# A second set of weight buffers for six panels of a gated linear unit

## The chip, the cores and the metric

The kernel runs on one core of one Trainium2 chip. The metric is device time in microseconds for one execution of the whole program, as the median of several runs. Engines that matter here are TensorE (PE in the profile, with PEld for its weight loads), VectorE (DVE), ScalarE (ACT), GpSimd (POOL) and the engine that issues transfers (SP).

## The reference

Two layers of a decoder trunk, sequence length 256, width 2048, all in float32. The first layer mixes tokens with an S5 state-space model, the second with a causal convolution module; both are followed by a SwiGLU feed-forward block. The change lies in the first layer, in the gated linear unit behind the S5 model:

```python
y = jax.nn.gelu(y + d_skip.astype(f32) * u.astype(f32)).astype(u.dtype)
vg = y @ w_glu                       # (256, 2048) @ (2048, 4096)
return vg[..., :d] * jax.nn.sigmoid(vg[..., d:])
```

Around each sub-layer stands `x <- LayerNorm(alpha * x + (1 + gate(c)) * sublayer(x * (1 + scale(c)) + shift(c)))`. The six vectors shift, scale and gate of a layer are the product of an activated vector `c` with a matrix of 2048 x 12288, so these conditioning weights have to be read from HBM as well, beside the weights of the layers.

## The kernel before

Every large product is made of panels, and a panel of units. A unit is a piece of 512 of the 2048 inner rows by 512 output columns of a weight matrix (1 MB). For the gated linear unit a panel is 256 columns of the value half and the matching 256 of the gate half; there are eight panels of four units.

The path of a unit (class `Unit`): `load_unit` takes a tile named `raw` and SP issues two transfers of 512 KB into it (L585). ACT casts it to the high half `whi` (L843), and DVE subtracts that from `raw` to make the low half `wlo` (L844). PE multiplies: 16 matmuls with `whi` (activations high and low), 8 with `wlo` (L902). `whi` and `wlo` have two buffers each. A panel's last unit is taken in two halves, one for each output bank. At the end of a panel ACT and DVE form the gate (`sg`), PE transposes it (`turned`, L919), and DVE adds it into the residual `X` (L1074).

Beside this runs `AdaQueue`: at a rate of about one step per unit it loads a conditioning row block of 1 MB into a tile named `rawa` (L686, issued by SP), and DVE adds it, scaled, into `adaacc` (L699 and L701). When a vector is complete, PE sums it over partitions (`adar`, L709) and turns it (`adat`, L717).

`raw` and `rawa` tiles come from one pool, `rawp`, of four buffers of 1 MB:

```python
rawp = ctx.enter_context(tc.tile_pool(name="raw", bufs=4))
...
raws = [rawp]
...
    r = raws[0].tile([P, 4, 512], F32, tag="raw", name="raw")
...
    raws.append(raws.pop(0))
```

`raws` is a list of pools; each weight load takes a tile from the first and moves that to the end of the list. `rawa` tiles always come from `rawp`. SP's queue is worked off in order; a transfer whose buffer is not free yet holds up what stands behind it. A planner puts the instructions of each engine in an order: it goes by program order, and takes by its own estimate of time the first that is ready. Only the PE order of panel 0 is written out by hand.

Before panel 0 ends, the S5 model's tiles in the fast memory are given up (`s5.work_ctx.close()` and `s5.mats_ctx.close()` in `s5_end`). The room is next used by the pool `f0`, opened ahead of panel 7, whose one large tile first holds the split input of the feed-forward block (`entry_raw`, class `Entry`, L974 to L981) and later the block's inner activations. `reuse_waits="tile"` says that a tile of a pool laid over older tiles waits for those tiles it lies on.

The loop over the eight panels is at L1551 and the lines behind it.

Of the kernel before, what the change touches and what calls it, by code (L numbers as in the profile page):

```python
# [504 lines left out]
def kernel(  # L505
# [11 lines left out]
    rawp = ctx.enter_context(tc.tile_pool(name="raw", bufs=4))  # L517
# [4 lines left out]
    def aux(name):  # L522
        return auxp.tile([P, 512], F32, tag="aux", name=name)
# [51 lines left out]
    raws = [rawp]  # L575
# [495 lines left out]
    def residual(y, gt, ch, stats=None):  # L1071

        for k in range(2):
            done = nc.vector.scalar_tensor_tensor(  # L1074
                out=X[:, ch + k], in0=y[:, k], scalar=gt[:, ch + k:ch + k + 1], in1=X[:, ch + k], op0=MUL, op1=ADD)
            if stats and stats.behind:
                with queue_behind([done]):
                    stats.behind.pop(0)()
        if stats is None:
            return  # L1080
        i, z = ch // 2, X[:, ch:ch + 2]
        if i == 0:
            later.put(1, lambda: stats.begin(z))
            later.put(1, lambda: stats.add(0, z))
            for p in range(1, 8):
                later.put(1 if p == 1 else 2 + p % 2, lambda p=p: stats.move(X[:, 2 * p:2 * p + 2]))
        elif i == 1 and later.todo:
            later.put(1, lambda: stats.add(1, z))
        else:
            stats.add(i, z)  # L1090

    def gated(wsrc, off, width, sp, then, entry=None, wide=True, **kw):

        segs = [(off, 256), (width + off, 256)]
        if entry:
            def from_entry(vs):
                for i in range(2):
                    entry_gated(vs[i], vs[2 + i], sp)
                then(vs[0][2])

            entry.panel(wsrc, segs, [(256, 256), (width + 256, 256)], kw["wp"], from_entry)
            ada.credit = -3.0
            return
        acc = gemm(wsrc, 0, NCH, segs, xh, banks=((0, 2), (1, 3)), wide=wide, **kw)
        t = sp.tile([P, 2, SEQ], F32, tag="sg", name="sg", bufs=2)
        for i, ab in enumerate(acc):
            nc.scalar.activation(out=t[:, i], in_=ab[:, 1], func=AF.Sigmoid)
            nc.vector.tensor_tensor(out=t[:, i], in0=ab[:, 0], in1=t[:, i], op=MUL)
        if wide:
            turning.put(2, lambda: turned([t[:, 0], t[:, 1]], 0, then))  # L1110
        else:
            then(t)
# [9 lines left out]
    def gu_cols(f):  # L1122
        return [(f * P, 256), (DFF + f * P, 256)]
# [399 lines left out]
    def entry_raw(fp):  # L1523
        t = fp.tile([P, 24, 2, SEQ], F32R, tag="f2", name="raw").rearrange("p a h b -> p (a h b)")
        return t[:, 0:2 * NCH * EW]
# [5 lines left out]
    with mctx:  # L1531
# [4 lines left out]
        def enter(name, stats, i, k, raw, pairs):  # L1536

            layer, j = (i, 3) if k == 0 else (i + 1, 0)
            ada.finish(layer, j)
            ada.finish(layer, j + 1)  # L1540
            g, b = ln_gb(i, k)
            hg, hb = fold(name, g, b, mod[layer][:, j + 1], mod[layer][:, j])
            e = Entry(sp, stats, raw, hg, hb, scaled(name + "xg", g, ALPHA), scaled(name + "xb", b, ALPHA))
            for p in range(pairs):
                later.put(1 + p // 2, lambda p=p: e.split(p))
            return e

        f0ctx = ExitStack()
        bank = auxp.tile([P, 512], F32, tag="ada", name="acc", bufs=1)
        first = {"acc": [b.rearrange("p (a b) -> p a b", b=SEQ) for b in (aux("acc"), bank)], "before": {1: last_scan, 2: lambda: held_back.append(s5.end), 3: s5_end}}  # L1550
        for i in range(8):  # L1551
            if i == 7:
                fp = f0ctx.enter_context(tc.tile_pool(name="f0", bufs=1, reuse_waits="tile"))
                raw = entry_raw(fp)
                entry = enter("f0", stats, 0, 0, raw, 7)
            with ExitStack() as order:
                if i == 0:
                    order.enter_context(tc.manual_schedule(engines={mybir.EngineType.PE}))
                gated(s5_w_glu[0], 256 * i, D, sp, lambda t, i=i: residual(t, mod[0][:, 2], 2 * i, stats), wp=wp, wide=i < 7,
                      ahead=(ffn_w_gu[0], gu_cols(0)) if i == 7 else None, **(first if i == 0 else {}))  # L1560
            if i == 1:
                held_back.clear()
            ada.rate = 1.05
            ada.hold = i == 6
            if i == 0:
                later.put(10, load_vectors)
# [237 lines left out]
```

## Time and profile before

| | us |
|---|---|
| median of 3 runs | 2275.47 |
| lowest and highest run | 2272.48, 2278.56 |
| profiled execution, its own time | 2271.02 |
| its span | 2269.2 |
| panels 1 to 6 in it, first matmul of panel 1 to first of panel 7 | 230.3 to 376.4 |
| PE busy in the span | 2212.5 |
| DVE busy | 1669.2 |
| ACT busy | 1018.8 |
| mean rate of the transfers over the span | 255 GB/s |

A row of a timeline gives the start, the time, the engine, the line of the kernel, the operation, what it writes and reads, the shapes and how many instructions were merged; a bracket at the end is idle time of that engine just before, and what ended it. SPq is SP's queue, and a row there is the issue of a transfer, not the transfer. A row of waits gives the total, the number of times and the longest. In the table of stretches each engine has its busy time with the number of instructions.

### The profile page before, as it was taken

The page shows a single profiled execution, that of the slowest core. Times are in us where ns is not written, and L with a number is a line of the kernel's source. Part 1 is how long each engine was busy: PE and PEld are TensorE (multiplying, and loading weights), DVE is VectorE, ACT ScalarE, POOL GpSimd, SP SyncE. Part 2 cuts the span into 40 slices and gives each one's busy share as a digit, 9 for nine tenths or more (in the row PEclk, how much of TensorE's full clock was granted, in tenths as well). Part 3 has the DMA queues.
Part 4 walks back from the last instruction along what each step waited for, and adds up shares of the span by engine and source line. Part 5 has one row for each costly group of instructions (what it writes and reads, how often), then busy time and mean ns, then how long its engine had stood idle before and what let it go on. Part 6 is the DMA issues. An engine that isn't in the chain of part 4 may idle for free.

```text
span 2269.2 us, 33415 instructions
## 1 busy us (share of the span) xinstructions
PE 2212.5 (97%) x13611; PEld 1798.0 (79%) x13611; DVE 1669.2 (74%) x1812; ACT 1018.8 (45%) x1238; POOL 157.4 (7%) x265
## 2 busy tenths in 40 slices
PE   7999999999999999999999998999999999999998
PEld 4556778988788888787897776898888888888888
DVE  8897898878777777777988788878755444555474
ACT  4775334644333333333455434556443333434343
POOL 5761000000000000000010110000000000000000
PEclk8999999999999999999999999999999999999999
DMA  9998899589998899998856775757865555555542
GB/s 332 343 324 276 300 355 310 178 314 324 316 330 322 319 329 326 317 324 318 311 161 198 227 211 198 252 196 235 284 223 186 185 190 191 188 191 186 189 165 92
DMA packets 380607, 579.48 MB, mean 255 GB/s; under 512 B 13875, under 2 KB 277939, under 8 KB 365987
## 3 DMA queue, kind: packets, MB, share of 16 engines
q1 hardware_dynamic: 379862, 576.82, 74.9%
q8 instruction: 107, 1.75, 0.3%
q0 software_dynamic: 352, 0.45, 0.1%
q14 instruction: 46, 0.38, 0.1%
q10 hardware_dynamic: 240, 0.08, 0.0%
HBM read 573.72 MB, written 3.57 MB: 254 GB/s over the span
## 4 chain that ended last, share of the span: by engine, by line
PE 75%; DVE 11%; DMA 7%; ACT 4%; issue 2%; SPq 0%; POOL 0%; POOLq 0%; DVEq 0%; ACTq 0%
PE acc L902 61%; PE acc L907 6%; DMA raw<-in_ffn_w_gu_dram 4%; DVE wlo L844 3%; ACT whi L843 2%; PE acc L1019 2%; PE turned L919 2%; DMA raw<-in_s_w_glu_dram 1%; DVE adaacc L701 1%; PE conv L1695 1%; DMA raw<-in_ada_w_dram 1%; PE ada L629 1%; PE y L499 1%; DVE pin L476 1%; PE adar L709 0%
## 5 line engine op out<-in xcount | busy, mean ns | idle before, releaser
L844 DVE TENSOR_TENSOR wlo<-raw,whi 128x2048 fp32r<-128x2048 f32 x344 | 788.9, 2294 | 467.4 <-ACT whi L843 462.8
L843 ACT CAST whi<-raw 128x2048 fp32r<-128x2048 f32 x344 | 655.5, 1906 | 814.6 <-PE acc L902 414.6
L902 PE MATMUL acc<-whi,h 128*128 128x512 f32 x3648 | 890.4, 393 | 7.9 <-ACT whi L843 7.6
L902 PEld LDWEIGHTS acc<-whi,h 128*128 128x128 f32 x3648 | 678.6, 188 | 160.7 <-ACT whi L843 12.8
L902 PE MATMUL acc<-wlo,h 128*128 128x512 f32 x1824 | 461.7, 390 | 0.8 <-DVE wlo L844 0.5
L902 PEld LDWEIGHTS acc<-wlo,h 128*128 128x128 f32 x1824 | 341.6, 188 | 73.9 <-DVE wlo L844 3.3
L902 PE MATMUL acc<-whi,f 128*128 128x512 f32 x1248 | 300.9, 391 | 0.0
L701 DVE SCALAR_TENSOR_TENSOR adaacc<-rawa,c_act,adaacc 128x2048 f32<-128x2048 f32 (+1 forms) x135 | 284.6, 2108 | 0.4
L902 PEld LDWEIGHTS acc<-whi,f 128*128 128x128 f32 x1248 | 232.8, 188 | 49.5 <-ACT whi L843 1.7
L902 PE MATMUL acc<-wlo,f 128*128 128x512 f32 x624 | 156.5, 389 | 0.0
L902 PEld LDWEIGHTS acc<-wlo,f 128*128 128x128 f32 x624 | 117.1, 188 | 24.4
L1625 POOL TENSOR_TENSOR lw<-fold,wtap 128x1024 f32<-128x1024 f32 x12 | 26.6, 2220 | 1056.6 <-PE acc L907 867.7
L629 PE MATMUL ada<-raw,c_rep 128*32 128x512 f32 (+1 forms) x576 | 68.9, 574 | 7.0 <-DMA raw<-in_ada_w_dram 4.9
L1256 ACT ACTIVATE fsg<-acc 128x256 f32<-128x256 f32 x84 | 31.6, 379 | 96.1 <-PE acc L902 96.1
L907 PE MATMUL acc<-h,whi 128*128 128x256 f32 x512 | 66.8, 285 | 3.4 <-ACT h L923 2.5
L907 PEld LDWEIGHTS acc<-h,whi 128*128 128x128 f32 x512 | 63.2, 191 | 8.0 <-ACT h L923 4.5
L1198 POOL CAST lnmh<-lno 128x2 fp32r<-128x2 f32 x1 | 0.2, 181 | 883.6 <-DVE lno L68 883.6
L1257 DVE TENSOR_TENSOR fsg<-acc,fsg 128x256 f32<-128x256 f32 x84 | 35.0, 419 | 15.5 <-ACT fsg L1256 15.5
L1695 PE MATMUL conv<-vs,lw 128*32 128x256 f32 x720 | 42.2, 381 | 0.1
L907 PE MATMUL acc<-f,whi 128*128 128x256 f32 x320 | 40.8, 284 | 0.0
L907 PEld LDWEIGHTS acc<-f,whi 128*128 128x128 f32 x320 | 39.4, 192 | 0.2
L476 DVE TENSOR_TENSOR_SCAN pin<-rho,pin 128x1024 f32<-128x1024 f32 x16 | 36.7, 2295 | 0.6
(352 smaller groups left out, 1831.0 us busy)
## 6 DMA issues: line engine op xcount, KB each, us to landing
raw<-in_ffn_w_gu_dram SPq DMA_DIRECT2D x352, 512.0 KB, 4.7
rawa<-in_ada_w_dram SPq DMA_DIRECT2D x128, 1024.0 KB, 5.5
raw<-in_ffn_w_down_dram SPq DMA_DIRECT2D x88, 1024.0 KB, 5.1
raw<-in_ada_w_dram SPq DMA_DIRECT2D x64, 1024.0 KB, 8.0
raw<-in_s_w_glu_dram SPq DMA_DIRECT2D x64, 512.0 KB, 5.8
raw<-in_cv_w_pw_dram SPq DMA_DIRECT2D x64, 512.0 KB, 5.6
raw<-in_cv_w_pw_dram SPq DMA_DIRECT2D x16, 1024.0 KB, 5.7
vs<-scr SPq DMA_DIRECT2D x40, 142.0 KB, 5.5
```

The costliest lines, as they stand in the source:

```text
L476: done = v.tensor_tensor_scan(out=z, data0=rh.rearrange("p q r c -> p (q r c)"), data1=z, initial=0.0, op0=MUL, op1=ADD)
L629: nc.tensor.matmul(acc[32 * (k % 4):32 * (k % 4) + 32, :], c_rep[:, kk, :], r[:, k, :], start=kk < 4, stop=kk >= NCH - 4)
L701: nc.vector.scalar_tensor_tensor(out=acc, in0=r[:, i], scalar=c_act[:, kk:kk + 1], in1=acc, op0=MUL, op1=ADD)
L843: m1 = nc.scalar.copy(out=self.hi[:, :kn], in_=r[:, :kn])
L844: m2 = nc.vector.tensor_tensor(out=self.lo[:, :kn], in0=r[:, :kn], in1=self.hi[:, :kn].bitcast(F32), op=SUB)
L902: nc.tensor.matmul(acc[bank].rearrange("p a b -> p (a b)"), x[:, bank * HALF:(bank + 1) * HALF], wt[:, k], start=first, stop=end)
L907: nc.tensor.matmul(acc[bank][:, i], wt[:, k, m * P:(m + 1) * P], x, start=first and i == 0, stop=end and i == 1)
L919: nc.tensor.transpose(b[:, o:o + HALF], u[t][:, c0 + k * P:c0 + (k + 1) * P], ident)
L1019: nc.tensor.matmul(acc[m][:, 0:EW], wt[:, k, m * P:(m + 1) * P], xx[:, 4 * u + k], start=u == 0 and n == 0, stop=u == 3 and n == len(order ...
L1256: nc.scalar.activation(out=t[:, i], in_=gv[:, 0], func=AF.Sigmoid)
L1257: nc.vector.tensor_tensor(out=t[:, i], in0=gv[:, 0], in1=t[:, i], op=MUL)
L1695: nc.tensor.matmul(acc[32 * q:32 * q + 32, :], lw[:, q, g, :], vs[:, q, 4 * g:4 * g + SEQ], start=g == 0, stop=g == n - 1)
```

## The change

Ahead of panel 1 a pool of four buffers, `raw6`, is opened in the room that the S5 model has left, and the list of pools becomes six entries long: the old pool twice, the new one four times. Ahead of panel 7 the list is set back to the old pool, the new one is closed, and `f0` is opened as before. Nothing else differs.

```diff
         first = {"acc": [b.rearrange("p (a b) -> p a b", b=SEQ) for b in (aux("acc"), bank)], "before": {1: last_scan, 2: lambda: held_back.append(s5.end), 3: s5_end}}
+        wide_raws = ExitStack()
         for i in range(8):
+            if i == 1:
+                raws[:] = [rawp] * 2 + [wide_raws.enter_context(tc.tile_pool(name="raw6", bufs=4, reuse_waits="tile"))] * 4
             if i == 7:
+                raws[:] = [rawp]
+                wide_raws.close()
                 fp = f0ctx.enter_context(tc.tile_pool(name="f0", bufs=1, reuse_waits="tile"))
                 raw = entry_raw(fp)
                 entry = enter("f0", stats, 0, 0, raw, 7)
```

## The prediction

> **What bounds the kernel now.** The page came first, for the whole run. Its span and its counts:
>
> ```profile
> span 2269.2 us, 33415 instructions
> PE 2212.5 (97%) x13611; PEld 1798.0 (79%) x13611; DVE 1669.2 (74%) x1812; ACT 1018.8 (45%) x1238; POOL 157.4 (7%) x265
> ```
>
> PE is busy in 2212.5 of 2269.2 us, so all that any prefetch can win in the whole run is 57 us, and most of that lies outside the stage that the change touches. The next view is busy time by stretch, cut at the first matmul of panel 1 (230.3), of panel 2 (253.4) and so on to panel 7 (376.4), with one stretch behind it; columns are the stretch, its length, the busy time of PE, PEld, DVE, ACT and POOL (with instruction counts), the granted clock, the share of DMA time and GB/s.
>
> ```profile
> 230.30:253.40 23.10, 23.10 (x105) 19.15 (x104) 23.03 (x25) 9.12 (x9) 0.00 (x0) 1.00 0.94 324
> 253.40:280.40 27.00, 24.82 (x105) 18.34 (x103) 19.92 (x17) 9.29 (x8) 0.00 (x0) 1.00 0.98 342
> 280.40:305.70 25.30, 24.87 (x117) 19.26 (x116) 23.51 (x26) 9.06 (x8) 2.56 (x5) 1.00 0.92 321
> 305.70:328.70 23.00, 22.88 (x100) 18.25 (x100) 20.68 (x15) 8.80 (x8) 0.00 (x0) 1.00 1.00 339
> 328.70:352.30 23.60, 22.94 (x101) 18.27 (x101) 20.80 (x15) 8.83 (x8) 0.00 (x0) 1.00 1.02 363
> 352.30:376.40 24.10, 23.96 (x112) 18.72 (x112) 20.69 (x14) 10.53 (x9) 0.00 (x0) 1.00 1.01 350
> 376.40:400.00 23.60, 23.60 (x200) 23.60 (x198) 19.00 (x32) 14.72 (x25) 0.00 (x0) 1.00 0.75 240
> ```
>
> Panels 1 to 6 take 146.1 us, and PE idles there 0 + 2.18 + 0.43 + 0.12 + 0.66 + 0.14 = 3.53 us. Three things are nearly full at once: PE, DVE in panels 1 and 3, and the DMA engines from panel 4. The list of waits over 230.3 to 376.4 (total us, times, longest) says where a late weight goes:
>
> ```profile
> ACT whi L843 <- DMA raw<-in_s_w_glu_dram: 46.7, 17, 4.4
> ...
> PEld acc L902 <- ACT whi L843: 5.5, 7, 2.6
> ```
>
> ACT's cast to `whi` waits 46.7 us for weights, in 17 of the units, but ACT has that much slack: PE's weight loads, which run ahead of its matmuls, wait for it 5.5 us, and PE itself only in the two places shown below.
>
> **The wait that costs.** The timelines of PE, ACT, SP's queue and DVE around the longest one (start, length, instruction; in brackets the idle time before it):
>
> ```profile
> 253.44 3.79 PE L902 MATMUL acc<-whi,h 128*128 128x512 f32 x16
> 257.06 1.98 PE L902 MATMUL acc<-wlo,h 128*128 128x512 f32 x8
> ...
> 267.15 3.92 PE L902 MATMUL acc<-whi,h 128*128 128x512 f32 x16 [2.18 <-ACT whi L843]
> ```
>
> ```profile
> 265.20 1.90 ACT L843 CAST whi<-raw 128x2048 fp32r<-128x2048 f32 x1 [2.22 <-DMA raw<-in_s_w_glu_dram]
> ```
>
> ```profile
> 228.66 0.37 SPq L686 DMA_DIRECT2D rawa<-in_ada_w_dram  x1
> 231.07 0.92 SPq L585 DMA_DIRECT2D raw<-in_s_w_glu_dram  x2
> 234.59 0.37 SPq L686 DMA_DIRECT2D rawa<-in_ada_w_dram  x1
> ...
> 239.81 0.37 SPq L686 DMA_DIRECT2D rawa<-in_ada_w_dram  x1
> ...
> 256.70 0.92 SPq L585 DMA_DIRECT2D raw<-in_s_w_glu_dram  x2
> ```
>
> ```profile
> 241.90 1.28 DVE L701 SCALAR_TENSOR_TENSOR adaacc<-rawa,c_act,adaacc 128x1024 f32<-128x1024 f32 x1
> ...
> 246.13 2.29 DVE L844 TENSOR_TENSOR wlo<-raw,whi 128x2048 fp32r<-128x2048 f32 x1
> 248.34 1.28 DVE L701 SCALAR_TENSOR_TENSOR adaacc<-rawa,c_act,adaacc 128x1024 f32<-128x1024 f32 x1
> ...
> 255.40 3.92 DVE L701 SCALAR_TENSOR_TENSOR adaacc<-rawa,c_act,adaacc 128x1024 f32<-128x1024 f32 x3
> ```
>
> The third unit of panel 2 waits for its cast until 267.15, the cast for its weights until 265.20, and those were issued only at 256.70, when the first of three DVE adds from 255.40 (3.92 / 3 = 1.31 each) let go of a `rawa` tile at 256.7. Weights and conditioning rows share four buffers, and each buffer comes free by DVE, so a busy DVE holds back the loads.
>
> **The change, part by part.** The list of pools has six entries and rotates with each weight load: two `raw`, four `raw6`. So of the 24 loads of panels 1 to 6, 16 go to the new buffers and 8 stay in the old pool: the first two of panel 1, the last two of 2, the first two of 4, the last two of 5. No matmul, cast, subtraction, add or byte of DMA is added or removed; what moves is the moment at which SP may issue a load, and what SP waits on.
>
> *The third unit of panel 2* stays in the old pool. Each issue of now stands just behind a tile's release: five of them, all of the old pool, from 228.66 to 239.81, and the next release that isn't a new-pool tile's is the end of DVE's add, 248.34 + 1.28 = 249.62. Five conditioning loads take the first five, which they share with weight loads now, and this unit gets the one at 249.62: 7.1 us ahead of 256.70. At worst it lands as slowly as before (265.2 - 256.7 = 8.5 us), at 258.1, and its cast ends by about 260, where PE comes for it at 267.15 - 2.18 = 264.97. What is late next is DVE's half:
>
> ```profile
> 267.13 2.29 DVE L844 TENSOR_TENSOR wlo<-raw,whi 128x2048 fp32r<-128x2048 f32 x1 [1.23 <-ACT whi L843]
> ```
>
> DVE, now waiting for that cast from 267.13 - 1.23 = 265.90, needs 2.29 us from there, to 268.2, against PE's need 3.62 us into the unit (253.44 to 257.06), 268.6. So I take the whole 2.18 us.
>
> *The second unit of panel 5* has the next wait of this kind:
>
> ```profile
> 335.31 3.94 PE L902 MATMUL acc<-whi,h 128*128 128x512 f32 x16 [0.54 <-ACT whi L843]
> ```
>
> It comes from the new buffers, whose tile is free since panel 3: 0.54 us gone.
>
> *Starts that lose their overlap.* In the uninterrupted unit above, the `wlo` matmuls start 253.44 + 3.79 - 257.06 = 0.17 us before the end of the ones ahead; a start behind a wait loses that. PEld waits for the cast seven times, two of them counted above; the other five cost between 0 and what is left of the 5.5 us, 5.5 - 2.6 - 0.5 = 2.4. I take 5 x 0.17 = 0.85, by the row.
>
> Sum: 2.18 + 0.54 + 0.85 = 3.6 us. The bound above: all idle time of the six panels and all those starts, 3.53 + 2.4 = 5.9 us. The DMA engines give one of their own. Their answers for 230 to 376 and for 288 to 376:
>
> ```profile
> DMA packets 30589, 49.51 MB, mean 339 GB/s; under 512 B 1230, under 2 KB 27014, under 8 KB 28533
> ```
>
> ```profile
> DMA packets 19424, 31.05 MB, mean 353 GB/s; under 512 B 814, under 2 KB 17755, under 8 KB 17755
> ```
>
> At 353 GB/s the 49.51 MB take 140.3 us, 5.8 us under the 146.1 of now: deeper buffers fill holes of the DMA engines but don't make them faster. *The Trainium skill ("DMA: Bandwidth & Descriptors", Specifications) puts what one core gets from HBM at about 358 GB/s, which speaks against any larger gain; by it, an estimate, 138.3 us and at most 7.8 us, and the trace's 353 agrees with it.*
>
> *New waits.* The first load into `raw6` must wait for the S5 tiles that lay there. Their last reader is POOL:
>
> ```profile
> 226.89 2.28 POOL L1387 TENSOR_TENSOR h<-gl,h 128x256 fp32r<-128x256 f32 x1 [12.25 <-ACT h L1386]
> ```
>
> It ends at 229.17, before the 231.07 at which this load is issued now: nothing lost, up to 1.9 us of lead won. Behind a wait on SP stand all later loads; the conditioning load at 228.66 is ahead of it, and the next, with a buffer at 231.04 at the earliest, is not held. At the other end `f0` must wait for the readers of `raw6`:
>
> ```profile
> 369.32 2.29 DVE L844 TENSOR_TENSOR wlo<-raw,whi 128x2048 fp32r<-128x2048 f32 x1
> ```
>
> ```profile
> 377.40 0.21 ACT L974 CAST raw<-f0g 128x16 fp32r<-128x16 f32 x1
> ```
>
> The last unit of panel 6 is read until 371.6, and the first write into `f0` comes at 377.4: 5.8 us of cover. If that were gone, ACT's casts for panel 7 behind it would wait, one us for each us late. It is costed at 0. From 376.4 PE is full (23.60 of 23.60), so what is won arrives at the end.
>
> The profiled execution took 2271.0 us (span 2269.2 and 1.8 around it); less 3.6 it is 2267.4. The median of the runs is 2275.5, 4.4 above that execution, and on it the forecast is 2271.9.
>
> **The rivals.**
>
> *Rival 1: nothing reaches the end* (2275.5). For it: 8 loads still go through the shared pool, the stall at 267 sits at one of them, and DVE, which frees the buffers, is the fuller engine there (23.03 of 23.10 us in panel 1); if its half comes later than 268.6, the 2.18 us only change their cause. Against it: 7 us of lead at that load.
>
> *Rival 2: the weights overtake the conditioning rows* (slower). The planner passes over an instruction that isn't ready; PE's order shows it, one transpose of a group of four standing ahead of a unit and three behind it:
>
> ```profile
> 305.32 0.27 PE L919 MATMUL turned<-ident,sg 128*128 128x128 f32 x1
> ...
> 311.30 0.49 PE L919 MATMUL turned<-ident,sg 128*128 128x128 f32 x3
> ```
>
> Four free buffers at 229.2 may so put four loads of 1.05 MB (2.97 us each at 353 GB/s) ahead of the row load of 234.59. It would then land at 229.2 + 6 x 2.97 = 247.0 (one load under way, four weights, itself), its add, now at 241.90, 5.1 us late, and everything behind it on DVE too: the `wlo` of 246.13 would end at 253.5, where PE, which starts that unit one length (5.4 us) ahead of 253.44 and, as it is a panel's last, takes half of its `whi` first (3.62 / 2), wants it at 249.8. That is 3.7 us of PE, as much as the gain. One such pile-up gives 2275.6; from the second on the change is a loss, and one in each of the four rounds of the list gives 2271.9 + 4 x 3.7 = 2286.7. Against it: later, the new buffers come free one at a time, as DVE reads them. *The Trainium skill (the same page, Queues, rings and completion order) says that an engine takes descriptors in ring order, so an overtaken row does wait for all ahead of it; no run here shows this case.*
>
> *Rival 3: more than the stage's stalls*. All 5.9 us come (2269.6), and the planner, with other times, also orders work elsewhere better, where PE idles 57 - 3.5 = 53 us in all. Two more us there and it is 2267.6. Nothing in the profile says that it would go that way rather than the other.
>
> **How the numbers follow.** The forecast 0.50, rival 1 0.20, rival 2 0.15 and rival 3 0.15. The likeliest gives 2271.9. A change of 0.3%, about what a measurement of this kernel can tell from none, is 6.8 us: below 2268.6 lies rival 3's better part and the forecast's tail, 0.17; above 2282.3 rival 2 with three or four pile-ups, 0.12; within, 0.71. The range takes the bound of 5.9 us with some of rival 3 and the 3 us by which runs of before lie off their median, 2264, and rival 2 up to two pile-ups (2279.3), 2280.
>
> **What would show it.** Right: no wait of PE on `whi` near 267 and 335, ACT's 46.7 us far smaller, DMA at a full share already in panels 1 to 3, panel 7's first matmul about 142.5 us after panel 1's, everything behind unchanged. Rival 1: that distance is still 146, with PE waiting on `wlo`. Rival 2: on SP's queue four weight pairs in a row at 229, then DVE's `adaacc` waiting for `rawa`. Wrong altogether: a wait of ACT on the first write into `f0` at the end of panel 6, or a difference of more than 2 us that lies behind 376.

## The result and the profile after

The changed kernel takes 2266.33 us as the median of 12 runs (2263.96 to 2271.44), the kernel before 2272.71 us in 12 runs beside them (2267.71 to 2278.56). The ratio is 0.9976, with a 95% interval of 0.9966 to 0.9986: 5.4 us less, or 3.2 to 7.7 us (the two medians are 6.4 us apart). The change makes the kernel a little faster; the forecast was 3.6 us.

The profiled execution took 2266.68 us, 4.3 us less than that of before. The page of the changed kernel, its span and its counts:

```profile
span 2264.8 us, 33402 instructions
PE 2213.4 (98%) x13611; PEld 1798.1 (79%) x13611; DVE 1669.1 (74%) x1812; ACT 1018.9 (45%) x1238; POOL 157.4 (7%) x265
```

No work has gone. What went is time in which PE did nothing. The same view by stretch as before the prediction, for the changed kernel, cut at its own first matmuls of panels 1 to 7 (stretch, length, busy time of PE, PEld, DVE, ACT and POOL, granted clock, DMA share, GB/s):

```profile
229.64:252.86 23.22, 23.22 (x105) 19.09 (x104) 23.11 (x24) 9.26 (x9) 0.00 (x0) 1.00 1.04 378
252.86:276.19 23.33, 23.33 (x106) 18.37 (x104) 19.86 (x19) 9.19 (x8) 0.00 (x0) 1.00 0.87 297
276.19:301.59 25.40, 24.87 (x118) 19.32 (x116) 23.55 (x26) 9.19 (x9) 2.56 (x5) 1.00 1.02 357
301.59:324.42 22.83, 22.72 (x100) 18.22 (x100) 20.69 (x15) 8.82 (x8) 0.00 (x0) 1.00 1.03 375
324.42:347.26 22.84, 22.76 (x100) 18.21 (x100) 20.69 (x15) 8.71 (x8) 0.00 (x0) 1.00 0.90 321
347.26:371.38 24.12, 23.97 (x111) 18.72 (x112) 20.70 (x14) 10.57 (x9) 0.00 (x0) 1.00 1.08 364
```

Panels 1 to 6 take 371.38 - 229.64 = 141.7 us instead of 146.1. Panel 2 alone gives 27.00 - 23.33 = 3.7 of the 4.4 us and panel 5 gives 0.8; the other four stand within 0.2 us of where they were. PE's idle time in the six panels is 0 + 0 + 0.53 + 0.11 + 0.08 + 0.15 = 0.87 us instead of 3.53, and its busy time, the sum of the second column, fell from 142.57 to 140.87. Panel 1 starts 0.6 us earlier than before, and what stands behind panel 7's first matmul takes 0.6 us longer (2264.8 - 371.38 = 1893.4 against 2269.2 - 376.4 = 1892.8), so these two cancel.

PE's timeline in panel 2 and at the second unit of panel 5 (start, length, instruction), after:

```profile
252.86 3.79 PE L902 MATMUL acc<-whi,h 128*128 128x512 f32 x16
...
264.23 3.79 PE L902 MATMUL acc<-whi,h 128*128 128x512 f32 x16
...
275.21 1.05 PE L709 MATMUL adar<-adaacc,ones 128*32 128x512 f32 x4
...
330.24 3.91 PE L902 MATMUL acc<-whi,h 128*128 128x512 f32 x16
```

The third unit of panel 2 starts at 264.23 with no wait in a bracket, where 2.18 us stood; the second unit of panel 5 starts at 330.24 without the 0.54. There is one more difference, which the prediction did not have. The sums of a finished conditioning vector (`adar`, L709) stand in one place now, before in two. The same rows of the kernel before:

```profile
272.81 1.05 PE L709 MATMUL adar<-adaacc,ones 128*32 128x512 f32 x2
...
279.46 1.04 PE L709 MATMUL adar<-adaacc,ones 128*32 128x512 f32 x2
```

Two of these matmuls take as long as four, 1.05 us, so one place instead of two saves one stay of 273.79 - 272.81 = 0.98 us (its start to the next matmul's).

The queue of SP, after:

```profile
228.38 0.46 SPq L585 DMA_DIRECT2D raw<-in_s_w_glu_dram  x1
230.44 0.37 SPq L686 DMA_DIRECT2D rawa<-in_ada_w_dram  x1
...
233.96 0.37 SPq L686 DMA_DIRECT2D rawa<-in_ada_w_dram  x1
...
244.50 4.34 SPq L585 DMA_DIRECT2D raw<-in_s_w_glu_dram  x2
```

The row at 244.50 is the load of panel 2's third unit, issued at 256.70 before: 14.9 us after panel 1's first matmul instead of 26.4. (The row is long because SP's second issue in it took 3.9 us; both halves were started by 245.0.) The conditioning rows at 230.44 and 233.96 stood at 234.59 and 239.81. They went out earlier because the weight loads ahead of them no longer took the buffers that DVE gave back, and so DVE could add them earlier. DVE's timeline, after:

```profile
239.94 3.92 DVE L701 SCALAR_TENSOR_TENSOR adaacc<-rawa,c_act,adaacc 128x1024 f32<-128x1024 f32 x3
...
264.11 2.28 DVE L844 TENSOR_TENSOR wlo<-raw,whi 128x2048 fp32r<-128x2048 f32 x1
```

Three adds run at 239.94, where before one stood at 241.90 ahead of the `X` instructions. ACT's cast of the unit in question, after:

```profile
257.88 1.91 ACT L843 CAST whi<-raw 128x2048 fp32r<-128x2048 f32 x1 [2.47 <-DMA raw<-in_s_w_glu_dram]
```

It ends at 259.8 and DVE's half (264.11) at 266.4; PE needs that half 3.62 us into the unit, at 267.85. The waits over 229 to 372, after (total us, times, longest):

```profile
ACT whi L843 <- DMA raw<-in_s_w_glu_dram: 41.1, 16, 4.4
...
PEld acc L902 <- ACT whi L843: 2.8, 5, 0.8
...
PE acc L902 <- ACT whi L843: 0.5, 2, 0.3
```

ACT still waits 41.1 us for weights. What fell is the wait of PE and of its loads behind it: 5.5 to 2.8 us for the loads.

### The profile page after: what moved, and what is told of

Same layout as the page of the kernel before. It is cut to its first block, busy times and chain, and to the rows that moved or that the text cites. A ratio compares the mean times of both kernels' runs of the same rounds, so it can differ in the third digit from the quotient of the medians.

```text
span 2264.8 us, 33402 instructions
## 1 busy us (share of the span) xinstructions
PE 2213.4 (98%) x13611; PEld 1798.1 (79%) x13611; DVE 1669.1 (74%) x1812; ACT 1018.9 (45%) x1238; POOL 157.4 (7%) x265
## 3 DMA queue, kind: packets, MB, share of 16 engines
q8 instruction: 107, 1.75, 0.3%
## 4 chain that ended last, share of the span: by engine, by line
PE 80%; DVE 10%; DMA 4%; ACT 3%; issue 2%; SPq 0%; POOL 0%; POOLq 0%; DVEq 0%; ACTq 0%
PE acc L902 66%; PE acc L907 6%; DVE wlo L844 2%; PE acc L1019 2%; ACT whi L843 2%; PE turned L919 2%; DMA raw<-in_ffn_w_gu_dram 1%; PE conv L1700 1%; DMA raw<-in_s_w_glu_dram 1%; DVE adaacc L701 1%; PE ada L629 1%; DMA raw<-in_ada_w_dram 1%; DMA raw<-in_ffn_w_down_dram 1%; DVE pin L476 1%; PE y L499 1%
## 6 DMA issues: line engine op xcount, KB each, us to landing
vs<-scr SPq DMA_DIRECT2D x40, 142.0 KB, 5.6
```

## The experiments

The table has every kernel that was run. "Stage" is panels 1 to 6 in the profiled execution, first matmul of panel 1 to first of panel 7; "idle" is PE's idle time in it (its length less PE's busy time in the view by stretch). A ratio in a row is to the kernel before on the same chip. Single runs have no ratio.

| kernel | median us (runs) | ratio (95%) | stage us | idle us |
|---|---|---|---|---|
| before | 2272.71 (12) | 1 | 146.1 | 3.5 |
| before, second profile | 2272.55 (1) | | 144.9 | 2.1 |
| changed | 2266.33 (12) | 0.9976 (0.9966 to 0.9986) | 141.7 | 0.9 |
| changed, second profile | 2267.15 (12) | 0.9982 (0.9969 to 0.9994) | 143.2 | 2.2 |
| first_two | 2271.28 (12) | 0.9998 (0.9986 to 1.0010) | 143.9 | 2.8 |
| own_only | 2267.66 (10) | 0.9978 (0.9965 to 0.9990) | 141.3 | 0.7 |
| own_again | 2262.18 (1) | | 141.6 | 0.7 |
| two_bufs | 2267.19 (12) | 0.9984 (0.9974 to 0.9994) | 142.0 | 1.2 |
| four_ahead | 2267.48 (11) | 0.9984 (0.9975 to 0.9992) | 142.5 | 2.0 |
| sums_together | 2272.08 (12) | 1.0009 (0.9996 to 1.0022) | 147.6 | 4.5 |
| moves_on_pool | 2274.47 (12) | 1.0009 (0.9997 to 1.0022) | 148.4 | 5.3 |
| own_and_pool | 2273.09 (12) | 0.9998 (0.9988 to 1.0008) | 147.3 | 4.2 |
| light_adds | 2270.56 (1) | | 149.1 | 5.3 |
| half_rows | 2272.84 (1) | | 147.7 | 5.9 |

**How far a single profile can be read.** The kernel before and the changed one were profiled a second time, with nothing edited.

> The kernel before once more, for how far stretches of one kernel differ between profiled executions. Panels 1 to 6 at 146.1 within 0.3; the stretch from panel 7 to the end of the feed-forward's inner part 727 to 729 us if it is fixed by the program, several us away if it scatters.

> The changed kernel once more. Panels 1 to 6 at 141.7 us within 0.3, no wait of PE near the third unit of panel 2; time 3 to 6 us under before.

The same program's stage scatters by 1.2 us (before: 146.1, 144.9) and 1.5 us (changed: 141.7, 143.2), where 0.3 was expected. The means, 145.51 and 142.46, are 3.1 us apart, and the two pairs stand at 4.4 and 1.75. Of the 5.8 us between the spans of the second two profiles only those 1.75 lie in the stage; 1.4 lie ahead of panel 1 and 2.7 behind panel 7's first matmul, where nothing was edited. So the gain of the stage is known no better than 1.75 to 4.4 us, and how much of the 5.4 us of the runs it makes up stays open. In the second profile of the changed kernel a wait of PE is back, though not where it was; PE's timeline of that run:

```profile
277.42 3.94 PE L902 MATMUL acc<-whi,h 128*128 128x512 f32 x16 [1.17 <-ACT whi L843]
```

This is the first unit of panel 3, which has buffers of its own. In both profiles SP issues one half of its load at 262.4 and the other at 266.86, behind a conditioning row of 266.47 that waits for a shared buffer (DVE's half of panel 2's third unit, quoted above, lets go of one at 266.4); that half takes 7.2 us in the one and 8.5 us in the other. So even a load with a buffer of its own stands in SP's line behind those that have none.

**Panels 1 and 2 alone.** If the stall at panel 2's third unit is all, the new buffers are needed for these two panels only.

```diff
-            if i == 7:
+            if i == 3:
                 raws[:] = [rawp]
                 wide_raws.close()
+            if i == 7:
                 fp = f0ctx.enter_context(tc.tile_pool(name="f0", bufs=1, reuse_waits="tile"))
```

> The new buffers serve panels 1 and 2 only; from panel 3 on all loads come from the old pool again. If the gain is the load lead in panel 2, panel 2 stays at about 23.3 us (27.0 before), panel 5 goes back to 23.6 with its 0.54 us wait, panels 1 to 6 take 142.4 to 142.6 us, and the time is 5 us under before. If the buffers help all along (DMA holes in every panel), more than 1.5 us of the 4.4 come back.

The wait in panel 2 is gone, and a like one stands at panel 3's first unit. Rows of PE and of SP's queue in first_two:

```profile
281.61 3.96 PE L902 MATMUL acc<-whi,h 128*128 128x512 f32 x16 [1.85 <-ACT whi L843]
```

```profile
271.12 0.92 SPq L585 DMA_DIRECT2D raw<-in_s_w_glu_dram  x2
```

That unit's weights come from the old pool again and were requested only 10.5 us ahead of its start. With the lead given back, a wait of the same kind stands one panel later. How much of it is due to that is not shown, since 1.17 us stood at the same unit in the second profile of the changed kernel. Panel 5 is back at 23.5 us, about as expected. The time shows no gain (ratio 0.9998), where 5 us were expected; the stage is still 1.6 us shorter than the mean of before, and what stands ahead of panel 1 and behind panel 7's first matmul was 2.8 and 2.5 us longer in that execution than in the first of before, which no run explains.

**All loads in the new buffers, and only two of them.** In the change 8 of 24 loads stay in the shared pool. own_only sends all but the first two to `raw6`; two_bufs keeps the list and halves the buffers.

```diff
-raws[:] = [rawp] * 2 + [wide_raws.enter_context(tc.tile_pool(name="raw6", bufs=4, reuse_waits="tile"))] * 4
+raws[:] = [rawp] * 2 + [wide_raws.enter_context(tc.tile_pool(name="raw6", bufs=4, reuse_waits="tile"))] * 22
```

```diff
-...tc.tile_pool(name="raw6", bufs=4, reuse_waits="tile")...
+...tc.tile_pool(name="raw6", bufs=2, reuse_waits="tile")...
```

> All 22 loads from the third unit of panel 1 on use the new buffers, so that the old pool serves the conditioning rows alone. If the lead of the shared loads is already enough, panels 1 to 6 take the same 141.7 us within 0.3. If the eight shared loads still hold PE back, 0.5 to 1 us less.

> The kernel with own buffers for all 22 loads once more. Panels 1 to 6 at 141.3 us within 0.3; the stretch from panel 7 to the end of the feed-forward's inner part 724 us again if the program sets it, 726 to 729 if the earlier 724.0 was scatter.

> Two new buffers in place of four, the same rotation of six entries. If one more unit of lead does it, panel 2 stays at 23.3 us and the stage within 0.5 us of 141.7. If four buffers are needed, panel 2 goes back towards 27.0 and the wait on whi near 267 returns.

In own_only the waits over the stage show what the eight shared loads cost ACT:

```profile
ACT whi L843 <- DMA raw<-in_s_w_glu_dram: 10.9, 5, 3.7
```

ACT's wait falls from 41.1 to 10.9 us and the stage only from 141.7 to 141.3 (141.6 in own_again), within the scatter: with PE idle for 0.7 us there is almost nothing left to win. The transfers show it too. Two panels of own_only, the fourth and the sixth:

```profile
300.72:323.55 22.83, 22.73 (x100) 18.23 (x100) 20.68 (x15) 8.63 (x8) 0.00 (x0) 1.00 1.06 383
...
346.40:370.51 24.11, 23.97 (x112) 18.73 (x112) 20.70 (x14) 10.23 (x9) 0.00 (x0) 1.00 0.69 224
```

All loads of panel 6 are issued by 343.3, before it begins, and the DMA share falls to 0.69. Neither version can be told from the change in time (ratios 0.9978 and 0.9984 against 0.9976). Two extra buffers do nearly as well as four.

One thing is left open here. Behind panel 7's first matmul no kernel is edited, yet own_only is quicker there. The stretch from that matmul to the last down product, in before, in the changed kernel and in own_only (columns as above, one kernel each):

```profile
376.40:1128.20 751.80, 745.68 (x3580) 617.28 (x3578) 595.63 (x469) 319.26 (x294) 0.00 (x0) 1.00 0.88 307
```

```profile
371.40:1122.10 750.70, 745.54 (x3579) 617.12 (x3577) 595.23 (x469) 319.13 (x294) 0.00 (x0) 1.00 0.88 307
```

```profile
370.50:1118.10 747.60, 744.77 (x3580) 617.47 (x3579) 595.97 (x469) 319.54 (x294) 0.00 (x0) 1.00 0.87 309
```

PE idles 6.1, 5.2 and 2.8 us in it; the second profiles have 7.4, 4.7 and 3.4. Two profiles of each stand in the same order, so loads that are further ahead at the start of the feed-forward block may save some 1 to 4 us more in it. No run isolated that, and own_only's median does not show it.

**The slower rival, brought about.** four_ahead requests four units' weights together, ahead of the conditioning rows, as Rival 2 had feared of the planner.

```diff
-            r = load_unit(wsrc, k0, kn, segs)
+            r = early.pop(0) if early else load_unit(wsrc, k0, kn, segs)
...
+        def four_ahead():
+            for i, u in ((1, 2), (1, 3), (2, 0), (2, 1)):
+                early.append(load_unit(s5_w_glu[0], 4 * u, 4, [(256 * i, 256), (D + 256 * i, 256)]))
...
+                      **({"before": {1: four_ahead}} if i == 1 else {})
```

> The prediction's second rival made on purpose: the last two units of panel 1 and the first two of panel 2 are requested together, ahead of the conditioning rows. If overtaken rows cost what was reckoned, DVE waits about 5 us for a row near 242, PE about 3.7 us near 250, and the time is 3 to 4 us above the changed kernel. If DVE has slack for it, within 0.5 us of the changed kernel.

SP's queue did what Rival 2 says, and five rows stood behind the weights, four of them issued at once. Rows of SP's queue, of DVE and of PE in four_ahead:

```profile
220.15 14.38 SPq L585 DMA_DIRECT2D raw<-in_s_w_glu_dram  x10
234.62 15.12 SPq L686 DMA_DIRECT2D rawa<-in_ada_w_dram  x5
```

```profile
242.86 2.29 DVE L844 TENSOR_TENSOR wlo<-raw,whi 128x2048 fp32r<-128x2048 f32 x1 [2.55 <-ACT whi L843]
```

```profile
272.73 3.24 PE L902 MATMUL acc<-whi,h 128*128 128x512 f32 x13 [1.43 <-ACT whi L843]
```

DVE had one pause of 2.55 us there, for a cast and not for a row: the planner, by its own estimate of time, had put the adds behind the `wlo` instructions. PE paid 1.43 us in panel 2's last unit; the stage is 0.7 us longer than the first of the changed kernel and 0.7 us shorter than the second. The rows were slow to come: they landed 6.0 to 15.4 us after their issue. But the pile-up priced at 3.7 us costs nothing that these runs can tell from the changed kernel (ratios 0.9984 and 0.9976).

**The order alone.** In the change the planner also moved the sums to one place, the end of panel 2. sums_together puts them in one place in the kernel before, with its four buffers; there it is one unit later, in panel 3.

```diff
-            later.put(1, total)
+            later.put(2 if (layer, j) == (0, 3) else 1, total)
...
+                with queue_behind(newest_mm if (layer, j) == (0, 3) else []):
                     for b in range(nb):
                         nc.tensor.matmul(ps[32 * b:32 * b + 32, :], ones[:, 0:32], ...)
```

> The kernel before, with its old buffers, but PE makes both sums of the first conditioning vector at one place, as the changed kernel's order does. If part of the gain is that order and not the buffers, panels 1 to 6 take about 1.0 us less than 146.1 with the 2.2 us wait on whi near 267 still there, and the time is 1 us under before. If the sums hide anyway, 146.1 as before.

Panel 2 falls to 24.3 us, but panel 3, where the sums now stand, rises to 28.3, and PE waits for weights there. Its row:

```profile
293.63 5.52 PE L903 MATMUL acc<-whi,h 128*128 128x512 f32 x16 [1.03 <-ACT whi L844]
```

The time is 1.0009 of before (0.9996 to 1.0022), so the order alone brought nothing here. That it can't be kept without the buffers is not shown: the sums stood elsewhere than in the changed kernel, and in half_rows below the planner put them at the end of panel 2 with the old buffers.

**What holds the load back: DVE, or the transfers?** Three edits of the kernel before. moves_on_pool takes eight subtractions of a shift off DVE and gives them to GpSimd; own_and_pool does that and adds the buffers of own_only. light_adds leaves out every second add of the first conditioning vector. half_rows loads only half of that vector's rows and adds the same half twice, so that the adds stay and half of its bytes go.

```diff
-            nc.vector.tensor_tensor(out=z, in0=z, in1=bc(self.shift, 1, z.shape[1]), op=SUB)
+            (nc.gpsimd if self.on_pool else nc.vector).tensor_tensor(out=z, in0=z, in1=bc(self.shift, 1, z.shape[1]), op=SUB)
```

```diff
+                if (layer, j) == (0, 3) and i == 1:
+                    continue
```

```diff
+            n = 1 if (layer, j) == (0, 3) else rows
             nc.sync.dma_start(
-                r, ada_w[layer, k * rows * P:(k + 1) * rows * P, ...])
+                r[:, :n], ada_w[layer, k * rows * P:(k * rows + n) * P, ...])
...
-in0=r[:, i]
+in0=r[:, 0 if (layer, j) == (0, 3) else i]
```

> The kernel before, with its old buffers, but the eight subtractions of the shift from X in panel 1 run on GpSimd (DVE 5 us lighter). If the wait near 267 comes from buffers that a busy DVE gives back late, the load of panel 2's third unit is issued some 4 to 5 us earlier, the wait goes without any new buffer, and panels 1 to 6 take 2 to 3 us less than 146.1. If it comes from the DMA engines' speed, the wait stays at about 2 us.

> Both: own buffers for all 22 loads and the subtractions on GpSimd. If the two remedies are for one cause, they don't add: panels 1 to 6 at 141.3 within 0.4 (own buffers alone: 141.3). If DVE still holds PE, up to 1 us less.

> The kernel before with its old buffers and all its transfers, but every second add of the first conditioning vector is left out (its value is then not the reference's). DVE is 1.3 us lighter per unit in panels 1 and 2. If late buffers come from the busy DVE, the load of panel 2's third unit goes out 5 us or more ahead of where it does (26.4 us behind panel 1's first matmul), and the wait on whi ahead of that unit (2.2 and 1.1 us in two executions) is gone, with no new buffer. If the DMA engines are the limit, the wait stays.

> The kernel before with its old buffers and all its adds, but of the first conditioning vector only every second row block is read from HBM (the adds use it twice; the value is not the reference's): 0.5 MB less per unit, with DVE's work as before. If DVE's releases set the loads, that load still goes out about 26 us behind panel 1's first matmul and PE still waits there, 0.3 to 1.5 us. If the DMA engines set them, the wait is gone.

The load of panel 2's third unit on SP's queue and the unit's start on PE, first in light_adds, then in half_rows:

```profile
253.00 0.92 SPq L585 DMA_DIRECT2D raw<-in_s_w_glu_dram  x2
```

```profile
264.16 3.79 PE L904 MATMUL acc<-whi,h 128*128 128x512 f32 x16
```

```profile
257.81 0.92 SPq L585 DMA_DIRECT2D raw<-in_s_w_glu_dram  x2
```

```profile
265.19 3.93 PE L903 MATMUL acc<-whi,h 128*128 128x512 f32 x16 [1.43 <-ACT whi L844]
```

Counted from panel 1's first matmul (229.62 and 229.07) the load goes out after 23.4 us with fewer adds and after 28.7 us with fewer bytes, against 26.4 in both profiles of before. With fewer adds PE does not wait; with half the bytes of that vector it waits 1.43 us, although panel 1 then moves only 226 GB/s instead of 324. In each of them the wait of SP ahead of this load is ended by DVE. So DVE's releases set this load, and fewer bytes in the transfers do not bring it forward. The lead of 3.0 us is less than the 5 that were expected. With fewer adds DVE itself pauses twice in panel 1, for casts (0.95 and 2.05 us), so its adds are not all that sets this load; these runs do not separate what else does. Neither execution is quicker over the whole stage, since later waits come in (light_adds is 5.2 us longer than before in panels 5 and 6): these two say something of the place, not of the time.

moves_on_pool should have helped by the same reasoning, and did not. The groups of DVE over 230 to 280 us, first in before, then in moves_on_pool (busy us, mean ns), one subtraction of DVE while POOL works, the moved work on POOL, and the load of panel 2's third unit:

```profile
L701 DVE SCALAR_TENSOR_TENSOR adaacc<-rawa,c_act,adaacc 128x1024 f32<-128x1024 f32 x15 | 19.2, 1281 | 0.2
L844 DVE TENSOR_TENSOR wlo<-raw,whi 128x2048 fp32r<-128x2048 f32 x7 | 16.0, 2286 | 1.9 <-ACT whi L843 1.9
L764 DVE TENSOR_TENSOR X<-X,shift 128x512 f32<-128x512 f32 x8 | 5.0, 685 | 0.0
```

```profile
L701 DVE SCALAR_TENSOR_TENSOR adaacc<-rawa,c_act,adaacc 128x1024 f32<-128x1024 f32 x14 | 22.2, 1585 | 0.2
L845 DVE TENSOR_TENSOR wlo<-raw,whi 128x2048 fp32r<-128x2048 f32 x7 | 19.3, 2754 | 0.0
```

```profile
243.39 3.38 DVE L845 TENSOR_TENSOR wlo<-raw,whi 128x2048 fp32r<-128x2048 f32 x1
```

```profile
241.09 19.10 POOL L765 TENSOR_TENSOR X<-X,shift 128x512 f32<-128x512 f32 x8 [13.99 <-ACT shift L761]
```

```profile
254.59 0.92 SPq L585 DMA_DIRECT2D raw<-in_s_w_glu_dram  x2
```

DVE was rid of 5.0 us of work, and its other instructions took 7 x 0.468 + 14 x 0.304 = 7.5 us more. The means hide where: the three subtractions that fall into POOL's work took 3.4 us each, the other four 2.3 as before. So nothing was won: the load went out 254.59 - 228.20 = 26.4 us after panel 1's first matmul, as in before, and PE waited 1.30 us for DVE's half of the unit ahead and 1.46 for the cast of this one. Then the buffers do not help either. In own_and_pool PE waits in the same unit of panel 2:

```profile
271.44 5.53 PE L903 MATMUL acc<-whi,h 128*128 128x512 f32 x16 [2.39 <-ACT whi L844]
```

DVE's half of the unit before was late as well (PE waited 0.97 us for it), and the stage is 147.3 us against 141.3 in own_only.

## Why the prediction was right, and where it was off

*The forecast and its base.* The sign holds, and the size within the noise: 3.6 us was forecast, 5.4 (3.2 to 7.7) and, in the second comparison, 4.1 (1.4 to 7.0) were measured. The place holds for the two waits that were named; the stage as a whole gave 4.4 and 1.75 us in the two pairs of profiles. The absolute forecast of 2271.9 is 5.6 us above the 2266.33 measured. Half of that is the base: the three runs shown of before have a median of 2275.47, twelve have 2272.71. The other half is the gain, 6.4 us between the medians.

*The third unit of panel 2* (2.18 us): right in its result, wrong in its way. The load was to take the release at 249.62, 7.1 us ahead; it went out at 244.50, 11.6 us ahead counted from panel 1's first matmul, because the conditioning rows and with them the adds had moved forward. But more transfers were then under way, and it landed only at 257.8, 13 us after its issue. That is 28.2 us after panel 1's first matmul, where 258.1 - 230.28 = 27.8 was to be the worst case: the step "at worst it lands as slowly as before (8.5 us)" was wrong, and the longer lead made up for it. The cast ended at 259.8 ("about 260"). DVE's half ended 36.8 us after panel 1's first matmul, where 268.2 - 230.28 = 37.9 was reckoned.

*The second unit of panel 5* (0.54 us): right. PE idled 2.66 us less in the six panels, against 2.18 + 0.54 = 2.72. The nearness hides two small waits of the changed kernel (0.17 us in panel 3 and 0.33 at the start of panel 4) that offset others.

*Starts that lose their overlap* (0.85 us): PE's busy time fell by 1.70 us, of which 0.98 are the sums in one place; 0.72 is left for this term. The size is near, but not at the five starts that were priced. From one unit's `wlo` matmuls to the next unit's, the third unit of panel 2 takes 5.44 us instead of 7.91 and the second of panel 5 takes 5.81 instead of 6.62: 0.29 and 0.27 us more than their waits. The last unit of panel 2 gives about 0.2 more than the 0.98. So the lost overlap lay at the two waits already counted and beside the sums, and the five other starts gave about nothing in sum; five waits of PE's weight loads for casts are still there.

*Not in the sum:* those 0.98 us, an order that the planner chose with the new times. The stage's 4.4 us of the first pair are thus 2.66 + 0.72 + 0.98. That 3.6 us lies so near to what was measured is partly luck: two profiles of each kernel give 3.1 us in the stage, the largest wait, 2.18 us in the execution from which it was priced, is 1.12 us in the second profile of before, and the 0.98 us were no part of the sum.

*New waits:* right that those at the two ends of `raw6` cost nothing. The last reader of the S5 tiles, in the changed kernel:

```profile
226.26 2.28 POOL L1387 TENSOR_TENSOR h<-gl,h 128x256 fp32r<-128x256 f32 x1 [11.49 <-ACT h L1386]
```

It ends at 228.54. SP issued the first half of the load at 225.81, just behind DVE's write of `gl` (L1385, ended at 225.74), and the second at 228.38, straight behind a conditioning row. So SP waited for DVE and not for POOL, as far as the profile shows, and no row behind was held up; the load still had more lead than the 1.9 us that were named. At the other end, the last subtraction of panel 6's units on DVE, PE's first matmuls with that half, and the first write into `f0` on ACT, after:

```profile
364.31 2.28 DVE L844 TENSOR_TENSOR wlo<-raw,whi 128x2048 fp32r<-128x2048 f32 x1
```

```profile
368.07 1.07 PE L902 MATMUL acc<-wlo,h 128*128 128x512 f32 x4
```

```profile
372.39 0.21 ACT L974 CAST raw<-f0g 128x16 fp32r<-128x16 f32 x1
```

The subtraction ends at 366.6 and the write starts at 372.4: 5.8 us of cover, as the prediction had it, and ACT's write has no wait in a bracket. What the prediction did not look for is a new wait inside the stage, from SP's order: the 1.17 us at panel 3's first unit in the second profile.

*The bound by the transfers* (353 GB/s, at most 5.8 us): it was too low as a bound, though it decided nothing. Panels of the changed kernel reach 378 GB/s, of own_only 383; at 380, by this estimate, the 49.51 MB would take 130.3 us. The limit of the stage is PE's busy time (140.87 of 141.74 us), not the transfers. The Trainium skill ("DMA: Bandwidth & Descriptors", Specifications) gives about 358 GB/s for one core; these panels of 23 us are above that, and the measurement decides here.

*The rivals.* Rival 1 (nothing arrives) is refuted by the interval. Rival 2 was wrong in its mechanism and its price: the rows were not overtaken but went out earlier, and where four_ahead made them stand behind ten issues, the planner turned DVE's order round and PE lost nothing that can be measured instead of 3.7 us. The rule of ring order of the Trainium skill ("DMA: Bandwidth & Descriptors", Queues, rings and completion order), cited there, agrees with this run as far as it goes: the four rows issued at once behind the weights landed 9.7 to 15.4 us after their issue, where 5.1 us was the middle value in before. That DVE did not wait for them is the planner's doing. Rival 3 (other places gain as well) is partly so: 0.98 us of order inside the stage, and perhaps the feed-forward block (1.1 us shorter in both pairs of profiles), which stays open.

*The signs.* Right: no PE wait at the two places, panel 7 after 141.7 and 143.2 us (142.5 was named), and in the first pair no more than 0.6 us behind the stage. In the second pair 2.7 us lie behind it, more than the 2 us that were to speak against the whole account: 1.1 in the stretch up to the last down product, and most of the rest in the stretch whose clock differed (last section), in which nothing was edited. Wrong: ACT's 46.7 us were to be "far smaller" and are 41.1, and the DMA share was to be full in panels 1 to 3 and is 0.87 in panel 2. Both come from the eight loads left in the shared pool, as own_only shows, where ACT's wait is 10.9 us and panel 2's share 1.06, and neither costs PE anything much.

## What to carry to other kernels

When two streams share buffers and one in-order queue issues both, ask first which engine lets go of the buffers: here it was DVE, by an add at the load that stalled PE, and giving the weights room of their own let both streams go earlier. A wait on an engine with slack (ACT, 41 us) is no measure of what can be won; the idle time of the engine that sets the end (PE, 3.5 us in the stage) is. And before a gain of 0.2% is read from one pair of profiles, take a second one of each: the same program's stage differed by 1.2 to 1.5 us.

## What the runs showed of the hardware that was not expected

*Elementwise work on GpSimd slows VectorE.* While POOL worked for 19.1 us, DVE's subtraction of two tiles in float32 took 3.38 us instead of 2.29 (2754 ns on the mean of a window that POOL's work fills in part), and the add 1585 ns instead of 1281 on that mean. The two gate products in the midst of it, which read one of their two inputs from PE's accumulator, took 0.74 us together, as in before (0.75). One subtraction of 128x512 took 19.10 / 8 = 2.4 us on POOL, beside DVE's work, and 0.69 us on DVE. The Trainium skill ("SBUF — State Buffer", SBUF: two separate sides) says that the two engines share a pair of ports, which one of them holds for a whole instruction; DVE's slower rows agree with shared ports, and how long one engine holds them no run here shows.

*A wait of PE can cost more than its length.* In the row of own_and_pool above, 16 matmuls behind a wait of 2.39 us take 5.53 us instead of 3.92, while behind the 2.18 us of before they took 3.92. In light_adds 11 matmuls behind a wait of 2.37 us took 4.38 us, and the granted clock of those four microseconds was 0.59:

```profile
372.00:376.00 4.00, 4.00 (x12) 3.16 (x11) 3.35 (x2) 1.90 (x1) 0.00 (x0) 0.59 0.89 283
```

The length of the wait alone does not decide it: in sums_together a wait of 1.03 us had the same 5.52 behind it, and behind the same wait of 3.1 us in panel 0 stood 3.96, 5.5 or 6.6 us in different executions.

*The same stretch can run at another clock.* Behind the feed-forward block, 49 matmuls of both programs alike, in before and then in the changed kernel:

```profile
1394.30:1397.90 3.60, 3.60 (x49) 0.97 (x37) 2.42 (x11) 0.22 (x1) 0.00 (x0) 1.00 0.40 90
```

```profile
1388.20:1393.60 5.40, 5.40 (x49) 1.42 (x40) 2.42 (x11) 0.22 (x1) 0.00 (x0) 0.68 0.56 187
```

5.40 us instead of 3.60: this gave back 1.8 us of the profiled pair's gain, and in the second profiles the stretch that holds it, from the start of the last convolution matmul to that of the last matmul in the second block's entry panel, took 142.8 us in before and 141.1 in the changed kernel, the other way round.

*More transfers under way land later, at a higher rate.* The median time from issue to landing of a weight half, on the page of before and then of after:

```profile
raw<-in_s_w_glu_dram SPq DMA_DIRECT2D x64, 512.0 KB, 5.8
```

```profile
raw<-in_s_w_glu_dram SPq DMA_DIRECT2D x64, 512.0 KB, 10.2
```

The transfers of panel 1 moved 324 GB/s in before and 378 in the changed kernel; over the six panels it was 340 and 349.
